# The last pair of heads in a streaming encoder layer: branch B first, branch A last, with the last gates split between them

## The chip, the cores and the metric

The kernel runs on one core of one Trainium2 chip. The metric is device time in microseconds, from the first to the last instruction of one execution with what lies around it; a kernel's time is the median of its runs. The core has a matmul engine (TensorE, "PE" in the profile, with its weight loads as "PEld"), a vector engine (VectorE, "DVE"), an activation engine (ScalarE, "ACT"), a general engine (GpSimd, "POOL") and a queue engine (SyncE, "SP"), from which nearly all DMAs of this kernel are issued in order.

## The reference

The reference is one layer of a streaming encoder, for 2048 frames of a new stream (the prompt) and for 16 new frames of each of 8 running streams (the samples), whose 512 earlier frames lie in caches. All is float32.

```python
h, gate = adaln_modulate(x, c, norm_g, w_ada, b_ada)
qa, ka, va, za, qb, kb, vb, zb, ga, gb = project_inputs(h, w_in, pos)   # 4 x 512, 4 x 512, 2 x 1024 columns
# branch A: 4 heads; two softmaxes a head, over chunk-causal keys
p = softmax(mask(q1k1, q2k2) * 64 ** -0.5);  oa = (p[0] - lam * p[1]) @ va
# branch B: 8 heads; stick-breaking weights over strictly earlier keys
log_1m = where(mask, log_sigmoid(-z), 0)
log_a = log_sigmoid(z) + cumsum(log_1m, reverse=True) - log_1m
ob = where(mask, exp(log_a), 0) @ vb
# merge
ya = (rms_norm(oa, subln_g) * (1 - lam_init) * silu(za)) @ w_branch_a
yb = (ob * silu(zb)) @ w_branch_b
x = x + gate * ((sigmoid(ga) * ya + sigmoid(gb) * yb) @ w_out)
y = rms_norm(x, final_g)
```

Keys and values of both branches are outputs too. Queries and keys of branch A are rotated by position.

## The kernel before

The 2048 prompt frames are 16 tiles of 128 rows (`t` from 0 to 15); the 8 x 16 sample frames make a seventeenth tile, `NT`. Each float32 factor of a large product is split into two float16 parts, high and low, and three products of parts stand for one: a projection of a tile is 3 x 8 matmuls.

The start normalizes the frames and writes the transposed parts to `hT_d`. The first part of the kernel then runs over eight *units*. Unit `u` has a head index `h` and a kind: kind 0 is one head of branch A, kind 1 is a pair of heads of branch B. `prepare_unit` sets these at line 326 as `h, kind = u // 2, u % 2`, so A and B take turns and unit 7 is a B unit. A unit goes over the tiles in the order `NT`, 0, ..., 15 (`steps`). For each step `project` (matmuls at line 452) makes 512 columns of queries, keys, values and the gate path `z`. A unit may also have a slice of the 2048 merge gates `ga`, `gb` (`gate_piece`, line 528); `GATES` at line 63 gives the units 1, 3, 5 and 7, which are the B units, 512 columns each, and none to the A units. The result goes to `g_d`.

`scores` issues the attention of a tile. Branch A: scores (681, 682, the mask at 685) are scaled on DVE with a running maximum (582), Exp runs on ACT with the sum (128), DVE joins the two softmaxes (635), ACT and DVE split the weights into a high (306) and a low half (311), and a transposing DMA (604) turns them for the product with the values (738 to 740). Branch B: ACT makes two sigmoids of the scores (128), DVE runs a scan along the keys, last chunk first (658), POOL multiplies (664), ACT casts the high half (596), DVE subtracts for the low half (597), and the same DMA turns them for lines 742 and 743. B has two such jobs a tile, A one. For A `store` sums squares of the output into `osums`.

The order of the work is written out by the loop over `steps`. Projections are a list of pieces, `line`; at each step, the loop takes pieces up to a position that grows with the estimated time of the attention done so far (`duration`) and leads it by five steps (`LEAD`), and lays them between the score chunks. So the first tiles of a unit are projected while the last tiles of the unit before are scored, and after the last projection some tiles of attention are left. Products with values are issued later by a lag (`later_on`, `give`). A scheduler in the framework may still move instructions against its own model of time. The call `act` keeps ACT's table functions (Exp, Sigmoid) in the written order.

Beside this go side pieces: the preparation of the next unit's weights (`back`; fetch, sum of squares, split), norms of other weights and cached values (`spare`), cached keys (`cached`) and, in unit 7, cuts of the branch weights. A cached key block (32 of them, 512 KB each) is fetched, squared on ACT, split by POOL and DVE (`halve`) and stored to `keys_d`; one stage of this pipeline is a side piece. `keys_at` at line 1004 allows them in tiles 0 to 7 of units 1, 3 and 5 and in tiles 9 to 12 of units 2, 4 and 6, one at a step. Weights and blocks share one list of 16 buffers of 4 KB a partition, `free`. A unit with 512 gate columns holds eight of them, one without gates four.

`early_work` prepares the first two tiles of the second part near the end of unit 7: `inputs` loads outputs, gate paths and gates, takes the reciprocal roots of `osums` (all 16 tiles at once, the first time it is called) and applies sigmoids. The second part runs over the tiles 0 to 14, `NT`, 15: branch matmuls (1428), transposes (1265), the output matmuls (1457), the last norm and the store. Beside the first 13 of them the sampled streams' attention runs, unit by unit (`sample`, `lane`).

```python
    def keys_at(u, t):
        return u in (1, 3, 5) and t < 8 or u in (2, 4, 6) and 9 <= t < 13
```

Of the kernel before, what the change touches and what calls it, by code (L numbers as in the profile page):

```python
# [26 lines left out]
P = 128  # L27
# [6 lines left out]
NT = SEQ // P  # L34
# [27 lines left out]

GATES = [(u // 2 * 512, u % 2 * 512) for u in range(8)]

# [54 lines left out]
def layer_kernel(ctx: ExitStack, tc: tile.TileContext, a: dict):  # L119
# [63 lines left out]
    con = ctx.enter_context(tc.tile_pool(name="con", bufs=1))  # L183
# [139 lines left out]
    def prepare_unit(u, keep=None):  # L323


        h, kind = u // 2, u % 2
        U = dict(h=h, kind=kind, u=u, w=[], wg=[], bufs=[])
# [559 lines left out]
    def norms():  # L887
# [49 lines left out]

        def stages(k):
            if k > 1:
                halve()  # L940
            if 0 < k <= len(todo):
                square()
            if k < len(todo):
                fetch(*todo[k])

        return [lambda k=k: one(k) for k in range(len(srcs) + 1)], [lambda k=k: stages(k) for k in range(len(todo) + 2)]

# [53 lines left out]
    def norm_at(u, t):  # L1001
        return u < 7 and t < NT and (t >= 7 if u == 0 else t >= 9 or u == 6)

    def keys_at(u, t):
        return u in (1, 3, 5) and t < 8 or u in (2, 4, 6) and 9 <= t < 13

# [245 lines left out]
    L = {}  # L1252
# [8 lines left out]
    def transposed(x16, dst, half):  # L1261
# [4 lines left out]
        S.copy(out=dst[:, half * KT : (half + 1) * KT, :], in_=pt.rearrange("p (k n) -> p k n", n=P))  # L1266

    def inputs(t):

# [9 lines left out]
        begun.append(t)  # L1279
        r = L["orms"][:, 4 * t : 4 * t + 4] if t < NT else rsqrt(osums[:, NT, :], 4, P, tiny, "rA")  # L1280
        G.tensor_tensor(out=o[:, 0:nz], in0=o[:, 0:nz], in1=z[:, 0:nz], op=ALU.mult)  # L1281
# [51 lines left out]
    def early_work():  # L1333


        free.extend(units[7]["bufs"])

        def first(t):
            if "orms" not in L:
                L["orms"] = rsqrt(osums[:, 0:NT, :].rearrange("p t h -> p (t h)"), 4 * NT, P, con, "orms")  # L1340
            states[t] = inputs(t)
            if t == tiles[0]:
                turned(states[t])
                opened(states[t])

        def rest():
            L["g"], L["u"], (L["y"], L["y16"]) = free[0:4], free[4:6], free[6:8]

        return [branch_weight for _ in branch_weights] + [rest] + [lambda t=t: first(t) for t in tiles[0:2]]

    for n in range(len(steps) + 2):
        made, qk, side = [], [], []
        if n < len(steps):
# [6 lines left out]
            for fn in back[: -(-len(back) // max(1, (W_READY if u else W_READY + 2) - t % NT))]:  # L1360
                side.append((1.0, back.pop(0)))
            for todo, here in ((spare, norm_at), (cached, keys_at)):
                if todo and here(u, t):
# [179 lines left out]
```

## Time and profile before

| | |
|---|---|
| median of 3 runs | 2275.9 us (2274.01 to 2279.74) |
| profiled execution, its own time | 2280.78 us |
| its span | 2279.0 us |
| mean granted PE clock | 0.97 |
| PE / PEld busy | 92% / 49% |
| DVE / ACT / POOL busy | 75% / 71% / 31% |
| DMA moved | 445.30 MB, mean 195 GB/s |

A group's row gives line, engine, operation, what it writes and reads with its shapes, the count, then busy time in us and the mean in ns of one, then the idle time of the engine just before and what ended it. A row of stretches gives the window, its length, busy time and count for each engine, the granted clock of PE as a share of full speed, the busy share of the DMA engines and GB/s; restricted to one line of the kernel, it gives that line's instructions alone. A row in order of time gives the start, the length, engine, line and operation; a bracket at its end tells how long the engine was idle before and what it waited for. A busy PE isn't PE at its peak: matmuls overlap, so the pitch of their starts tells more than the mean of one.

### The profile page before, as it was taken

The page shows a single profiled execution, that of the slowest core. Times are in us where ns is not written, and L with a number is a line of the kernel's source. Part 1 is how long each engine was busy: PE and PEld are TensorE (multiplying, and loading weights), DVE is VectorE, ACT ScalarE, POOL GpSimd, SP SyncE. Part 2 cuts the span into 40 slices and gives each one's busy share as a digit, 9 for nine tenths or more (in the row PEclk, how much of TensorE's full clock was granted, in tenths as well). Part 3 has the DMA queues.
Part 4 walks back from the last instruction along what each step waited for, and adds up shares of the span by engine and source line. Part 5 has one row for each costly group of instructions (what it writes and reads, how often), then busy time and mean ns, then how long its engine had stood idle before and what let it go on. Part 6 is the DMA issues. An engine that isn't in the chain of part 4 may idle for free. (4 is left out here: it accounts for less than half of the span.)

```text
span 2279.0 us, 41771 instructions
## 1 busy us (share of the span) xinstructions
PE 2086.9 (92%) x14752; PEld 1122.3 (49%) x14752; DVE 1716.8 (75%) x3795; ACT 1617.6 (71%) x3228; POOL 701.4 (31%) x610
## 2 busy tenths in 40 slices
PE   5998899999999899899999989998997789899998
PEld 3654455554555455455554545554553444444443
DVE  4658768778886787988688788877778777767753
ACT  3967777888887687888677788866778566556541
POOL 1223014446411444642044355302335212211211
PEclk8999999999999999999999999999998799999999
DMA  9777658998796999978888899655677899888321
GB/s 329 271 234 186 160 134 213 197 222 193 201 244 155 221 210 196 211 195 215 193 213 204 200 217 230 172 130 138 153 156 155 203 292 239 221 214 224 122 106 47
DMA packets 805827, 445.30 MB, mean 195 GB/s; under 512 B 537354, under 2 KB 744506, under 8 KB 805104
## 3 DMA queue, kind: packets, MB, share of 16 engines
q1 hardware_dynamic: 804668, 442.24, 78.5%
q8 instruction: 115, 1.88, 0.3%
q14 instruction: 96, 0.79, 0.1%
q10 hardware_dynamic: 948, 0.39, 0.1%
HBM read 228.82 MB, written 86.02 MB: 138 GB/s over the span
## 5 line engine op out<-in xcount | busy, mean ns | idle before, releaser
L664 POOL TENSOR_TENSOR sc_p<-sc_p,sc_n 128x127 f32<-128x127 f32 (+7 forms) x192 | 319.2, 1664 | 701.7 <-DVE sc_n L658 529.6
L452 PEld LDWEIGHTS <-hs 128*128 128x128 f16 x3120 | 293.4, 99 | 332.4 <-DMA hs<-hT_d 15.5
L452 PE MATMUL ps_mm<-wa,hs 128*128 128x512 f16 x1590 | 389.8, 384 | 9.5 <-DMA hs<-hT_d 8.6
L452 PE MATMUL ps_mm<-wb,hs 128*128 128x512 f16 x1530 | 376.9, 381 | 5.8 <-DMA hs<-hT_d 4.8
L528 PE MATMUL ps_t<-wb,hs 128*128 128x512 f16 x1224 | 290.7, 380 | 1.3 <-DVE qst L556 1.0
L658 DVE TENSOR_TENSOR_SCAN sc_n<-ps_s,sc_n,zero_t 128x512 f32<-128x512 f32 x192 | 245.4, 1278 | 48.9 <-ACT ps_s L128 44.2
L681 PE MATMUL ps_s<-k,qst 128*128 128x512 f16 (+3 forms) x640 | 226.0, 354 | 46.3 <-DVE sc_n L658 31.3
L597 DVE TENSOR_TENSOR sc_n<-sc_p,sc_n 128x128 f16<-128x128 f32 (+7 forms) x192 | 212.6, 1111 | 49.3 <-ACT sc_n L596 49.2
L128 ACT ACTIVATE sc_p<-ps_s,usc 128x512 f32<-128x512 f32 (+3 forms) x320 | 204.7, 640 | 61.5 <-PE ps_s L682 48.4
L528 PEld LDWEIGHTS <-hs 128*128 128x128 f16 x1632 | 156.5, 98 | 184.1 <-DVE qst L556 3.4
L682 PE MATMUL ps_s<-k,qst 128*128 128x512 f16 (+3 forms) x640 | 226.0, 354 | 0.0
L596 ACT CAST sc_n<-sc_p 128x128 f16<-128x128 f32 (+7 forms) x192 | 155.3, 814 | 68.6 <-POOL sc_p L664 68.0
L128 ACT ACTIVATE ps_s<-ps_s,usc 128x512 f32<-128x512 f32 (+3 forms) x328 | 199.6, 609 | 0.0
L1457 PE MATMUL ps_o<-wo,wb 128*128 128x512 f16 x816 | 182.9, 379 | 0.7 <-ACT wb L1266 0.7
L742 PE MATMUL ps_o<-v,wt 128*128 128x128 f16 x1088 | 131.4, 224 | 18.8 <-DMA wt<-sc_n 18.7
L582 DVE TENSOR_SCALAR_CACHE_REDUCE sc_n<-ps_s,usc 128x512 f32<-128x512 f32 (+3 forms) x160 | 106.4, 665 | 46.5 <-PE ps_s L685 30.8
L1457 PEld LDWEIGHTS <-wb 128*128 128x128 f16 x816 | 78.1, 98 | 94.5 <-issue 1.2
L738 PE MATMUL ps_o<-v,wt 128*128 128x128 f16 x544 | 100.4, 222 | 25.8 <-DMA wt<-sc_n 25.6
L743 PE MATMUL ps_o<-v,wt 128*128 128x64 f16 x1088 | 123.6, 197 | 0.0
L658 DVE TENSOR_TENSOR_SCAN sc_n<-ps_s,zero_t 128x128 f32<-128x128 f32 (+3 forms) x128 | 104.0, 813 | 25.5 <-ACT ps_s L128 24.9
L742 PEld LDWEIGHTS <-wt 128*128 128x128 f16 x1088 | 101.1, 101 | 44.2 <-DMA wt<-sc_n 24.8
L582 DVE TENSOR_SCALAR_CACHE_REDUCE sc_p<-ps_s,usc 128x512 f32<-128x512 f32 (+3 forms) x160 | 106.2, 664 | 21.3 <-PE ps_s L682 14.2
(369 smaller groups left out, 4425.7 us busy)
## 6 DMA issues: line engine op xcount, KB each, us to landing
hs<-hT_d SPq DMA_DIRECT2D x130, 512.0 KB, 4.4
g_d<-gt SPq DMA_DIRECT2D x68, 256.0 KB, 4.8
out_dram<-pr SPq DMA_DIRECT2D x204, 64.0 KB, 4.0
wa<-in_w_in_dram SPq DMA_DIRECT2D x34, 256.0 KB, 5.6
o_d<-o SPq DMA_DIRECT2D x136, 64.0 KB, 1.9
wa<-g_d SPq DMA_DIRECT2D x17, 512.0 KB, 5.5
wb<-g_d SPq DMA_DIRECT2D x17, 512.0 KB, 4.8
hs<-o_d SPq DMA_DIRECT2D x17, 512.0 KB, 5.5
```

The lines of the kernel that those rows point to most:

```text
L128: i = S.activation(**kw)
L452: T.matmul(box["p"], box["h"][:, hi, k, :], U["w"][k][:, wi, :], start=(n == 0), stop=(n == 3 * KT - 1))
L528: T.matmul(box["g"][:, 0:gw], box["h"][:, hi, k, :], U["wg"][k // per][:, k % per, wi, :], start=(j == 0), stop=(j == 3 * KT - 1))
L582: V.tensor_scalar(out=dst[:, lo : lo + n], in0=p[:, 0:n], scalar1=sc_pos, scalar2=None, op0=ALU.mult, op1=ALU.max, accum_out=job["mx"][:, ...
L596: S.copy(out=hi, in_=src)
L597: V.tensor_tensor(out=lo, in0=src, in1=hi, op=ALU.subtract)
L658: V.tensor_tensor_scan(out=dst[:, lo : lo + n][:, ::-1], data0=src[:, 0:n][:, ::-1], data1=zero_t[:, 0:1].to_broadcast([P, n]), initial=fi ...
L664: G.tensor_tensor(out=p[:, 0:m], in0=p[:, 0:m], in1=n[:, 1 : m + 1], op=ALU.mult)
L681: T.matmul(p[:, 0:n], qst[:, c, :], kk[:, c, 0:n], start=True, stop=False)
L682: T.matmul(p[:, 0:n], qst[:, 2 + c, :], kk[:, c, 0:n], start=False, stop=not diag)
L742: T.matmul(po[:, c * P : (c + 1) * P], wt[:, wj, :], vt[:, c, :, :], start=first, stop=False)
L1457: T.matmul(po, st["y"][:, yi * 8 + k, :], wo[j * 4 + k // 2][:, wi, k % 2, :], start=(n == 0), stop=(n == 3 * KT - 1))
```

## The change

Three tables replace three rules. `UNITS` gives head and kind of each unit; it differs from the rule before in the last two, where unit 6 is now the B pair of head index 3 and unit 7 the A head 3. `GATES` now gives, in units 6 and 7, 256 columns each of the last 512 gate columns; units 1, 3 and 5 keep 512. With 256 columns `prepare_unit` puts four slices of the weights in one staged buffer instead of two, and a unit holds six buffers. `KEYS_AT` replaces `keys_at` with five stretches, (unit, first tile, tile after the last): the 32 key blocks are dealt out as 7, 6, 7, 6, 6, and each stretch fills and empties its own pipeline, `n + 2` stages laid evenly over its tiles. Unit 5 has no stretch any more, and that of unit 6 lies in tiles 0 to 7.

Since the sums of unit 7 are now those of branch A, `inputs` takes the reciprocal roots from `roots`, in two groups of eight tiles, each computed when its first tile is prepared. The sampled streams' units follow `units`, so there too the last two change places.

```diff
-GATES = [(u // 2 * 512, u % 2 * 512) for u in range(8)]
+KEYS_AT = [(1, 0, 8), (2, 9, 13), (3, 0, 8), (4, 9, 13), (6, 0, 8)]
+UNITS = [(0, 0), (0, 1), (1, 0), (1, 1), (2, 0), (2, 1), (3, 1), (3, 0)]
+GATES = [(0, 0), (0, 512), (512, 0), (512, 512), (1024, 0), (1024, 512), (1536, 256), (1792, 256)]
...
-        h, kind = u // 2, u % 2
+        h, kind = UNITS[u]
...
-        def stages(k):
+        def stages(n, k):
             if k > 1:
                 halve()
-            if 0 < k <= len(todo):
+            if 0 < k <= n:
                 square()
-            if k < len(todo):
-                fetch(*todo[k])
...
+            if k < n:
+                fetch(*todo.pop(0))
+
+        halved = {}
+        for i, (u, first, last) in enumerate(KEYS_AT):
+            n = -(-len(todo) * (i + 1) // len(KEYS_AT)) - -(-len(todo) * i // len(KEYS_AT))
+            for k in range(n + 2):
+                halved.setdefault((u, first + k * (last - first) // (n + 2)), []).append(lambda n=n, k=k: stages(n, k))
...
-    def keys_at(u, t):
-        return u in (1, 3, 5) and t < 8 or u in (2, 4, 6) and 9 <= t < 13
...
+    def roots(t):
+
+        g = t // 8
+        if ("orms", g) not in L:
+            L["orms", g] = rsqrt(osums[:, g * 8 : g * 8 + 8, :].rearrange("p t h -> p (t h)"), 32, P, con, f"orms{g}")
+        return L["orms", g][:, t % 8 * 4 : t % 8 * 4 + 4]
...
-        r = L["orms"][:, 4 * t : 4 * t + 4] if t < NT else rsqrt(osums[:, NT, :], 4, P, tiny, "rA")
+        r = roots(t) if t < NT else rsqrt(osums[:, NT, :], 4, P, tiny, "rA")
...
-            if "orms" not in L:
-                L["orms"] = rsqrt(osums[:, 0:NT, :].rearrange("p t h -> p (t h)"), 4 * NT, P, con, "orms")
             states[t] = inputs(t)
...
-            for todo, here in ((spare, norm_at), (cached, keys_at)):
+            side += [(1.0, fn) for fn in cached.pop((u, t), [])]
+            for todo, here in ((spare, norm_at),):
```

More of the change, by code (lines that the diff above doesn't have):

```diff
@@ L936, in norms @@
         todo = [(name, h, i) for name in ("ak", "bk") for h in range(4) for i in range(4)]
-        def stages(k):
+        def stages(n, k):
             if k > 1:
                 halve()
-            if 0 < k <= len(todo):
+            if 0 < k <= n:
                 square()
-            if k < len(todo):
-                fetch(*todo[k])
-        return [lambda k=k: one(k) for k in range(len(srcs) + 1)], [lambda k=k: stages(k) for k in range(len(todo) + 2)]
+            if k < n:
[5 more added lines that the diff above has]
+                halved.setdefault((u, first + k * (last - first) // (n + 2)), []).append(lambda n=n, k=k: stages(n, k))
+        return [lambda k=k: one(k) for k in range(len(srcs) + 1)], halved
     steps = [(u, t) for u in range(8) for t in [NT] + list(range(NT))]
```

## The prediction

> **What bounds the kernel now.** I read the page first, then the tail of the eighth unit in order of time, then busy time by stretches, then groups by shape.
>
> ```profile
> span 2279.0 us, 41771 instructions
> ...
> PE 2086.9 (92%) x14752; PEld 1122.3 (49%) x14752; DVE 1716.8 (75%) x3795; ACT 1617.6 (71%) x3228; POOL 701.4 (31%) x610
> ```
>
> PE is the bound as a whole. Where it isn't, time can be won. To cut the span into units of attention I use ACT's table loads: one stands where Exp (branch A) follows Sigmoid (branch B) or the reverse. The row of 1552.25 ends unit 6 (A) and starts unit 7 (B).
>
> ```profile
> 1384.86 1.28 ACT L128 ACT_TABLE_LOAD   x1
> ...
> 1552.05 0.19 ACT L128 ACTIVATION_READ_ACCUMULATOR sc_n<-sc_n,nm 128x1 f32 x1
> 1552.25 1.28 ACT L128 ACT_TABLE_LOAD   x1
> 1553.55 0.31 ACT L128 ACTIVATE r<-szs 128x128 f32<-128x128 f32 x1
> ```
>
> ```profile
> core 0: us, PE busy (x) PEld busy (x) DVE busy (x) ACT busy (x) POOL busy (x), PEclk, DMA share, GB/s
> 967.30:1137.50 170.20, 165.14 (x1146) 90.47 (x1144) 134.27 (x380) 132.33 (x298) 38.83 (x44) 0.98 0.82 202
> 1137.50:1384.90 247.40, 231.03 (x1669) 125.00 (x1668) 202.13 (x338) 195.09 (x404) 120.49 (x94) 0.99 0.91 207
> 1384.90:1552.30 167.40, 160.12 (x1122) 87.32 (x1119) 133.73 (x373) 126.57 (x289) 36.82 (x41) 1.00 0.71 172
> 1552.30:1727.20 174.90, 167.74 (x1159) 89.46 (x1158) 133.99 (x226) 121.87 (x256) 60.10 (x50) 0.99 0.69 153
> 1727.20:1771.70 44.50, 28.72 (x238) 15.95 (x236) 41.75 (x51) 36.95 (x64) 27.83 (x15) 0.73 0.71 144
> 1771.70:1792.50 20.80, 8.04 (x97) 7.48 (x97) 16.58 (x29) 11.64 (x16) 6.64 (x5) 0.60 0.79 162
> ```
>
> These are units 4 (A), 5 (B), 6 (A), and 7 (B) in three pieces: up to its last projection matmul, up to its last score matmul ("tail"), up to the first matmul of the second part ("drain"). Up to 1727.2 PE idles 5 to 16 us in a unit. In the tail DVE is busy 41.75 of 44.5 us (94%) while PE is granted 0.73 of its clock and idles: three tiles of B's attention are left and no projection to lay beside them. In the drain PE waits for transposes:
>
> ```profile
> 1725.70 1.46 PE L528 MATMUL ps_t<-wb,hs 128*128 128x512 f16 x6
> ...
> 1771.33 0.38 PE L682 MATMUL ps_s<-k,qst 128*128 128x512 f16 x1
> 1773.12 0.23 PE L742 MATMUL ps_o<-v,wt 128*128 128x128 f16 x1 [1.41 <-DMA wt<-sc_n]
> ...
> 1777.75 0.29 PE L742 MATMUL ps_o<-v,wt 128*128 128x128 f16 x1 [3.78 <-DMA wt<-sc_n]
> ...
> 1788.24 0.29 PE L742 MATMUL ps_o<-v,wt 128*128 128x128 f16 x1 [4.84 <-DMA wt<-sc_n]
> ...
> 1792.50 0.97 PE L1428 MATMUL ps_mm<-wa,wb 128*128 128x512 f16 x3
> ```
>
> So I add up five pieces: 247.4 + 167.4 + 174.9 + 44.5 + 20.8 = 655.0 us.
>
> **The change, part by part.** Prices of one operation:
>
> ```profile
> L658 DVE TENSOR_TENSOR_SCAN sc_n<-ps_s,sc_n,zero_t 128x512 f32<-128x512 f32 x192 | 245.4, 1278 | 48.9 <-ACT ps_s L128 44.2 <-DVE sc_n L658 0.5
> ...
> L597 DVE TENSOR_TENSOR sc_n<-sc_p,sc_n 128x1024 f16<-128x1024 f32 x80 | 118.0, 1475 | 28.6 <-ACT sc_n L596 28.5
> ...
> L582 DVE TENSOR_SCALAR_CACHE_REDUCE sc_n<-ps_s,usc 128x512 f32<-128x512 f32 x112 | 83.4, 745 | 22.4 <-PE ps_s L682 14.6 <-PE ps_s L685 7.0 <-DMA wt<-sc_n 0.6
> ...
> L635 DVE SCALAR_TENSOR_TENSOR sc_p<-sc_n,r,sc_p 128x1024 f32<-128x1024 f32 x40 | 51.7, 1296 | 0.0
> ...
> L311 DVE SCALAR_TENSOR_TENSOR sc_n<-sc_p,r,sc_n 128x1024 f16<-128x1024 f32 x40 | 51.7, 1292 | 4.5 <-ACT sc_n L306 4.5
> ...
> L306 ACT ACTIVATE sc_n<-sc_p,r 128x1024 f16<-128x1024 f32 x40 | 46.2, 1154 | 27.7 <-DVE sc_p L635 27.3
> ...
> L128 ACT ACTIVATE sc_p<-sc_p,nm 128x1024 f32<-128x1024 f32 x40 | 45.8, 1145 | 40.2 <-DVE nm L614 40.1
> ...
> L311 DVE SCALAR_TENSOR_TENSOR wa<-wa,csc,wa 128x1024 f16<-128x1024 f32 x24 | 37.4, 1558 | 8.3 <-POOL wa L308 8.3
> ...
> L128 ACT ACT_TABLE_LOAD x15 | 19.2, 1283 | 0.2
> ```
>
> *Tail.* For the last tile B needs on DVE 8 scans and 4 subtractions: 8 x 1.278 + 4 x 1.475 = 16.1 us. A needs 8 evacuations, 2 joins and 2 low halves: 8 x 0.745 + 2 x 1.296 + 2 x 1.292 = 11.1 us. The ratio is 0.69, so the tail of 44.5 becomes 30.5 us. ACT isn't the new bound: 4 exponentials and 2 high halves are 4 x 1.145 + 2 x 1.154 = 6.9 us a tile. A also sends one job of transposes a tile instead of two, so SP has half as many to issue there. Ends: 26 us if A's DVE work runs without a gap beside the shorter queue (1.5 us off each of three tiles), 44.5 if something other than DVE held the tail. I take 30.5 since DVE's 94% leaves room for little else.
>
> *Drain.* After A's last evacuation come four exponentials (4.6), join (1.3), high half (1.2), low half (1.3), a transpose (4.3 to landing, the median of its row below) and the second segment behind it (1.3): about 14 us, then 24 blocks of products. The first two tiles of the second part are prepared in the same stretch, as before, and their sigmoids stand between A's exponentials in ACT's fixed order, so tables are switched there: Exp to Sigmoid, back, and again, where B's Sigmoid needed none. One switch is 1.28 us by its rows, with the neighbours within 0.02 us on both sides. If the three lie on the path the drain is 14 + 2 + 3.8 = 20, if none does 16; I take 18 against 20.8, since the first falls under the last evacuations. The Trainium skill, "ScalarE: Activation LUTs", section "What ACT_TABLE_LOAD costs", adds a drain of about 1.4 us to the load's 1.28 us; by that the drain would end near 20 and the whole change would bring 2 us less. The rows of 1384.86 and 1552.25 show no such second part.
>
> ```profile
> wt<-sc_n SPq DMA_TRANSPOSE x288, 4.3
> ```
>
> *Gates.* 17 tiles x 24 matmuls of 512 columns become twice as many of 256. Pitches:
>
> ```profile
> 2161.52 5.19 PE ps_mm L1428 x24
> ```
>
> ```profile
> 1000.93 0.27 PE L681 MATMUL ps_s<-k,qst 128*128 128x256 f16 x1
> 1001.04 0.27 PE L682 MATMUL ps_s<-k,qst 128*128 128x256 f16 x1
> ```
>
> 0.216 and 0.11 us: 816 x 0.11 - 408 x 0.216 = +1.6 us of PE in all. ACT gets 17 more evacuations, SP 17 more stores of gates; both have room (below). The weights are fetched in the same bytes, with two staged blocks for each half instead of four for one.
>
> *Where PE's work goes.* By line the projections of the three units stand so (446, 375 and 267 matmuls), and 512-column gates 288, 109 and 301:
>
> ```profile
> 1137.50:1384.90 247.40, 109.38 (x446) 42.11 (x446) 0.99 0.91 207
> 1384.90:1552.30 167.40, 88.32 (x375) 35.05 (x375) 1.00 0.71 172
> 1552.30:1727.20 174.90, 65.00 (x267) 24.66 (x267) 0.99 0.69 153
> ```
>
> ```profile
> 1137.50:1384.90 247.40, 66.73 (x288) 27.49 (x288) 0.99 0.91 207
> 1384.90:1552.30 167.40, 24.80 (x109) 10.49 (x110) 1.00 0.71 172
> 1552.30:1727.20 174.90, 70.97 (x301) 28.88 (x299) 0.99 0.69 153
> ```
>
> Unit 5: (446 - 288) / 24 = 6.6 tiles of unit 6 are projected beside it, each now with gates: 158 x 0.11 = +17.4 us of PE. Against that go eight blocks of cached keys (on DVE a low half of 1.56 us and four tiny operations, some 2 us each), and DVE's share falls to that of the A units, where PE idles 5 to 7 us instead of 16. 231 + 17.4 + 7 - 2 (less half clock) = 253 us. Ends: 248 (no idle) and 265 (idle as before). I take 253.
>
> Unit 6, now B: 408 projections and 408 half gates, 133 us at the pitches above, with a unit's own scores and products, 62 us (231.0 - 734 x 0.216 = 72.5 in unit 5's row, 160.1 - 484 x 0.216 = 55.6 in unit 6's; the mean, less 2 of half clock): PE 195. DVE: unit 5's 202, less eight blocks of keys (16), plus six (12), less 3 that lie between its last score and the table load: 195; ACT, with two squares fewer, about 192. POOL's load becomes that of unit 5's row, half of the time; unit 7 takes over the rotations of A's queries and keys and keeps room, and SP issues 48 transposes in unit 6 for 24. Three engines at nearly the same load; this is the doubtful term. The nearest stretch is B's last tiles beside projections without gates:
>
> ```profile
> 1330.00:1410.00 80.00, 70.86 (x539) 38.48 (x538) 71.93 (x122) 66.49 (x139) 48.83 (x44) 0.96 0.97 204
> ```
>
> DVE is at 90% there. 195 / 0.90 = 217 us against 167.4. Ends: 202 (PE with an A unit's 7 us of idle) and 239 (DVE at unit 5's 82%).
>
> Unit 7, now A: the remaining 234 projections and 250 half gates, 78 us, with 42 us of products and scores up to the tail (167.7 - 568 x 0.216 = 45 in its row, less an estimated 3 since A's late products came over from unit 6 and B's are fewer), and 6 of idle: 126 us. DVE has room.
>
> *Keys.* The 32 blocks and their loads and stores on SP are the same, in 42 stages for 34, since each stretch fills and empties itself. Unit 5 loses its eight (counted above). Units 2 and 4 get six blocks in four tiles where they had four: two stages a tile. There PE already waits once:
>
> ```profile
> 1050.00:1065.00 15.00, 10.95 (x72) 6.22 (x70) 9.74 (x27) 11.26 (x28) 1.22 (x1) 0.77 0.96 228
> ```
>
> DMA is at 0.96 in this stretch. I count the crowding at nothing, as PE is full in the next tiles and DMA stands at 0.82 over the unit; without that cover it is 4 us in each of two units.
>
> *Reciprocal roots.* They are computed for eight tiles at a time: 15 small DVE operations twice. The first set waits for sums of tiles 0 to 7 of the last unit, stored several tiles before; what stands behind it on DVE is the preparation of the second part's first tile, which PE needs only after the drain. The second set lies in the second part, some 3 us of DVE beside PE. Counted at nothing; at most 3 us. Order of the sampled streams' units: the last two change places, the same work.
>
> *Sum.* 253 + 217 + 126 + 30.5 + 18 = 644.5, against 655.0: 10.5 us less. The profiled execution took 2280.78 us (span 2279.0), 4.9 above the median of 2275.9; the difference carries over to the median: 2265.
>
> **The rivals.**
> 1. Slower: unit 6 is held by DVE and ACT. If DVE reaches only the 82% of unit 5's row, the unit takes 239 us and the sum is 11.5 over the present: 2287. For it: B's scan, POOL multiply, ACT cast and subtraction form one chain, and PE no longer has the long gates that cover it. Against: 90 to 94% where DVE was the bound. It decides from 227 us (86%), and shows as slower from 234 us on.
> 2. No change: the idle of unit 5 stays at 16 us (+9), because it comes from small tiles' latency and late loads, not from DVE. Then 2274. Crowded keys would lead to the same place (+8).
> 3. More: unit 6 runs like an A unit, PE-bound at 202 us: 2250.
>
> **How the numbers follow.** Likeliest 0.45, its own range 2259 to 2271; rival 1 0.2, rival 2 0.2, rival 3 0.15. What this measurement can tell from no change is about 0.3%, 6.8 us: faster means below 2269. The likeliest case lies there but for a tenth, and all of rival 3: 0.56; with rival 2 and the rest, same 0.22; slower 0.22. The range that leaves out 2 in 10 goes from 2250 to 2286, the last just short of rival 1's point.
>
> **What would show it.** The stretch from the last projection matmul to the last score matmul should be near 30 us, with evacuations (L582) instead of scans; the drain 16 to 20 us with two or three table loads; no table load between units 5 and 6; from the load that opens unit 5 to the one before unit 7 some 470 us, and PE idle there of 25 to 30 us. The forecast is wrong if that span is over 485, if DVE waits for ACT and POOL in unit 6, or if the tail isn't shorter though DVE has less to do.

## The result and the profile after

The changed kernel takes 2297.1 us (median of six runs, 2292.8 to 2302.7) against 2275.9 us: a ratio of 1.0093, 95% interval 1.0073 to 1.0112. It is slower by about 21 us, where 2265 us (2250 to 2286) was forecast. The profiled execution took 2301.77 us, its span 2300.0, with a mean granted PE clock of 0.964 for 0.970. Lines of the first part stand two further down than before (line 682 is now 684), lines of the second part by five or more (1428 is 1439).

The page of the kernel after, span and busy time:

```profile
span 2300.0 us, 42681 instructions
...
PE 2107.5 (92%) x15162; PEld 1172.9 (51%) x15162; DVE 1714.3 (75%) x3817; ACT 1622.6 (71%) x3246; POOL 688.3 (30%) x611
```

The page hardly differs: 408 of the 410 more matmuls are the halved gates, and PE is busy 20.6 us longer while the span grew by 21. "Busy" counts a matmul at half clock as a long one, so this is no sign of more work. The stretches show the place. First the kernel before, busy time by stretches for units 2 and 3, which the prediction did not show (length, then busy time and count on PE, PEld, DVE, ACT and POOL, granted clock, DMA share, GB/s):

```profile
551.90:720.50 168.60, 163.05 (x1147) 89.54 (x1148) 133.50 (x379) 131.50 (x299) 38.52 (x43) 1.00 0.82 204
720.50:967.30 246.80, 228.87 (x1654) 123.66 (x1653) 201.84 (x336) 195.27 (x404) 119.33 (x93) 0.99 0.91 205
```

The same view of the kernel after: units 2, 3 and 4, units 5 and 6 together, then unit 7 up to its last projection matmul, its tail and the drain:

```profile
551.40:735.60 184.20, 171.20 (x1150) 92.96 (x1151) 137.47 (x390) 133.76 (x303) 39.83 (x45) 0.95 0.80 198
735.60:982.50 246.90, 230.74 (x1648) 124.48 (x1645) 199.43 (x332) 194.70 (x400) 116.11 (x92) 0.99 0.89 200
982.50:1165.90 183.40, 171.93 (x1172) 94.10 (x1173) 139.27 (x392) 135.72 (x308) 39.75 (x46) 0.97 0.80 194
1165.90:1620.50 454.60, 429.12 (x3320) 256.87 (x3318) 378.26 (x620) 366.04 (x760) 202.06 (x157) 0.98 0.84 191
1620.50:1775.70 155.20, 140.42 (x1104) 89.48 (x1102) 104.62 (x293) 90.09 (x214) 36.31 (x42) 0.97 0.56 135
1775.70:1794.70 19.00, 11.99 (x84) 7.16 (x83) 17.49 (x42) 13.64 (x25) 1.27 (x1) 0.91 0.51 127
1794.70:1813.40 18.70, 6.09 (x54) 5.25 (x53) 14.84 (x38) 18.46 (x23) 0.00 (x0) 0.52 0.38 82
```

Unit 2 went from 168.6 to 184.2 us (+15.6) and unit 4 from 170.2 to 183.4 (+13.2). Unit 3 did not move. Units 5 to 7 fell from 655.0 to 647.5 (-7.5), and the second part is the same, 486.5 and 486.6 us. 15.6 + 13.2 - 7.5 = 21.3. So by the stretches the swap and the split of gates, on which the forecast spent its terms, are not where the time came from: it came from the two units whose cached keys now run two stages a tile.

The 7.5 us aren't idle time that was filled. PE is busy 8.0 us less in units 5 to 7 (587.6 for 595.7), because matmuls run elsewhere: unit 4 holds 26 more than before (1172 for 1146), and the second part 98 more (3177 for 3079, busy 448.1 us for 440.0).

Unit 2 has nearly the same matmuls as before (1150 and 1147), but PE idles 13.0 us instead of 5.6 and is busy 8.2 us longer at a granted clock of 0.95 for 1.00. In stretches of 10 us around the stages of keys, the kernel before:

```profile
630.00:640.00 10.00, 8.29 (x64) 4.83 (x61) 8.76 (x28) 9.22 (x25) 1.33 (x1) 1.00 1.11 286
640.00:650.00 10.00, 8.77 (x80) 5.48 (x78) 7.78 (x22) 8.79 (x24) 1.22 (x1) 1.00 0.90 219
650.00:660.00 10.00, 10.00 (x49) 4.57 (x48) 9.45 (x25) 8.56 (x20) 1.12 (x1) 1.00 0.76 184
660.00:670.00 10.00, 9.99 (x81) 5.74 (x80) 10.00 (x33) 8.12 (x20) 1.12 (x1) 1.00 1.01 258
```

and after:

```profile
631.00:641.00 10.00, 8.56 (x73) 5.19 (x72) 8.52 (x31) 6.66 (x15) 2.56 (x3) 1.00 0.85 180
641.00:651.00 10.00, 6.39 (x39) 3.65 (x38) 5.66 (x16) 5.62 (x14) 1.12 (x1) 0.88 1.07 261
651.00:661.00 10.00, 7.23 (x40) 3.98 (x39) 8.16 (x23) 9.90 (x25) 1.12 (x1) 0.67 0.80 215
661.00:671.00 10.00, 10.00 (x72) 5.57 (x70) 6.63 (x20) 6.20 (x14) 2.24 (x2) 0.94 0.97 229
671.00:681.00 10.00, 6.33 (x37) 3.13 (x34) 6.03 (x15) 5.49 (x15) 0.00 (x0) 0.92 0.81 247
681.00:691.00 10.00, 9.89 (x52) 4.64 (x52) 5.84 (x20) 4.72 (x10) 1.12 (x1) 0.74 0.93 236
```

DMA is loaded about alike. What is new is that PE, DVE and ACT go slack together (in the stretches from 641 and from 671), and that the granted clock falls to 0.67 to 0.94 behind the gaps. All three waiting at once suggests that one thing is late for all. The order of time on SP's queue and on ACT (the bracket gives the idle time before an instruction and what ended it):

```profile
640.35 0.43 SPq L914 DMA_DIRECT2D wa<-in_cache_a_k_dram  x1
```

```profile
645.38 1.06 ACT L288 ACTIVATE junk<-wa 128x1024 f16<-128x1024 f32 x1 [5.11 <-DMA wa<-in_cache_a_k_dram]
```

The block of keys is issued at 640.35, and ACT, whose order is fixed, stands 5.11 us before its square. Behind the square on ACT are the casts and copies from which PE's next transposes and scores start. The waits of the stretch 631 to 691 (what waited, for what, total, times, longest):

```profile
ACT junk L288 <- DMA wa<-in_cache_a_k_dram: 5.1, 1, 5.1
...
ACT junk L288 <- DMA wb<-in_cache_a_v_dram: 2.7, 1, 2.7
...
PE ps_s L227 <- ACT junk L288: 3.4, 2, 2.6
...
PE ps_s L683 <- DVE csc L926: 2.6, 1, 2.6
```

Line 227 is the small matmul that adds a block's sums of squares over the partitions; it stands in PE's order, so PE waits for the square too. Line 683, a score, waits for line 926, which reads that sum out of `ps_s`, the buffers that the scores are written to. The load, the square, the sum and its reading form one chain through SP's queue, ACT, PE and DVE, each in its order. Before, neither of PE's two waits stood in unit 2; but ACT waited for loads of blocks there too, in the stretch 616 to 676:

```profile
ACT junk L286 <- DMA wa<-in_cache_a_k_dram: 3.7, 3, 1.9
```

So the chain is seen, and PE's waits in it (3.4 + 2.6 us) are new. How much of the 28.8 us hangs on the late load, the experiments have to tell.

### The profile page after: what moved, and what is told of

It is laid out like the page before. It is cut to its first block, busy times and chain, and to the rows that moved or that the text cites. A ratio compares the mean times of both kernels' runs of the same rounds, so it can differ in the third digit from the quotient of the medians.

```text
span 2300.0 us, 42681 instructions
## 1 busy us (share of the span) xinstructions
PE 2107.5 (92%) x15162; PEld 1172.9 (51%) x15162; DVE 1714.3 (75%) x3817; ACT 1622.6 (71%) x3246; POOL 688.3 (30%) x611
## 5 line engine op out<-in xcount | busy, mean ns | idle before, releaser
L666 POOL TENSOR_TENSOR sc_p<-sc_p,sc_n 128x127 f32<-128x127 f32 (+7 forms) x192 | 309.3, 1614 | 612.7 <-DVE sc_n L660 580.9
L454 PEld LDWEIGHTS <-hs 128*128 128x128 f16 x3120 | 294.2, 99 | 333.1 <-issue 17.2
L454 PE MATMUL ps_mm<-wb,hs 128*128 128x512 f16 x1530 | 377.1, 384 | 13.3 <-DMA hs<-hT_d 13.2
L530 PE MATMUL ps_t<-wb,hs 128*128 128x512 f16 (+1 forms) x1530 | 295.2, 341 | 1.5 <-ACT qst L558 0.9
L530 PEld LDWEIGHTS <-hs 128*128 128x128 f16 x2040 | 198.6, 99 | 158.5 <-issue 12.2
L495 POOL TENSOR_TENSOR rot<-pr,rope 128x256 f32<-128x256 f32 x68 | 55.6, 817 | 280.8 <-ACT pr L468 141.6
L740 PE MATMUL ps_o<-v,wt 128*128 128x128 f16 x544 | 106.3, 230 | 28.5 <-DMA wt<-sc_n 28.4
```

What stands on the lines that cost most here:

```text
L454: T.matmul(box["p"], box["h"][:, hi, k, :], U["w"][k][:, wi, :], start=(n == 0), stop=(n == 3 * KT - 1))
L530: T.matmul(box["g"][:, 0:gw], box["h"][:, hi, k, :], U["wg"][k // per][:, k % per, wi, :], start=(j == 0), stop=(j == 3 * KT - 1))
L666: G.tensor_tensor(out=p[:, 0:m], in0=p[:, 0:m], in1=n[:, 1 : m + 1], op=ALU.mult)
```

## The experiments

Stage lengths below are of one profiled execution each, between table loads and the marks of the prediction. Where the code of a stretch is the same they differ by some 3 us (unit 2 in after and keys_only, or in late_b and late_swap; units 5 to 7 in after, spread and quarter), and by up to 10 us in the second part (482 to 493). Ratios are to the kernel before on the same chip.

A stretch doesn't hold the same matmuls in every kernel, since projections move across its ends. So the last two columns give an estimate of what is left of units 2 and 4 without them, called net: the length less the time of the stretch's own matmuls at the pitches that these traces show at full clock (0.216 us for 512 columns, 0.162 for 384, 0.109 for 256, 0.056 for 128, 0.028 for 64).

| kernel | ratio, 95% interval | unit 2 | unit 4 | 5+6 | 7 with tail and drain | 5 to 7 | unit 2 net | unit 4 net |
|---|---|---|---|---|---|---|---|---|
| before | 1 | 168.6 | 170.2 | 414.8 | 240.2 | 655.0 | 8.1 | 10.0 |
| after | 1.0093 [1.0073, 1.0112] | 184.2 | 183.4 | 454.6 | 192.9 | 647.5 | 24.1 | 18.8 |
| keys_only | 1.0071 [1.0047, 1.0095] | 181.4 | 182.5 | 411.8 | 235.1 | 646.9 | 21.3 | 17.8 |
| spread | 1.0068 [1.0044, 1.0092] | 176.3 | 181.6 | 457.8 | 192.9 | 650.7 | 16.3 | 21.6 |
| split_noswap | 1.0106 [1.0083, 1.0129] | 175.3 | 179.0 | 445.2 | 215.8 | 661.0 | 15.4 | 19.0 |
| swap_nosplit | 1.0271 [1.0244, 1.0298] | 175.0 | 180.4 | 467.7 | 232.4 | 700.1 | 15.0 | 20.4 |
| quarter | 1.0035 [1.0022, 1.0047] | 172.6 | 175.7 | 459.9 | 191.0 | 650.9 | 13.7 | 15.7 |
| no_norms | 1.0072 [1.0048, 1.0095] | 179.5 | 178.8 | 478.9 | 182.5 | 661.4 | 14.1 | 12.4 |
| four | 1.0070 [1.0051, 1.0089] | 171.2 | 178.7 | 462.0 | 194.5 | 656.5 | 11.3 | 19.0 |
| b_only | 1.0014 [0.9998, 1.0030] | 165.7 | 161.7 | 476.7 | 180.2 | 656.9 | 8.3 | 5.0 |
| prefetch | 1.0055 [1.0038, 1.0072] | 174.0 | 171.1 | 474.1 | 181.3 | 655.4 | 14.4 | 11.4 |
| late_b | 1.0056 [1.0043, 1.0069] | 170.8 | 177.6 | 421.9 | 235.9 | 657.8 | 11.2 | 18.5 |
| late_b3 | 1.0051 [1.0031, 1.0071] | 165.9 | 164.5 | 420.9 | 237.3 | 658.2 | 8.5 | 7.0 |
| late_swap | 1.0035 [1.0022, 1.0047] | 173.9 | 176.7 | 470.1 | 181.7 | 651.8 | 14.1 | 17.6 |

By the last columns the change costs 16.0 us in unit 2 and 8.8 in unit 4 beyond the matmuls; the other 4.3 us of unit 4 are matmuls that moved there (164.6 us at the pitches for 160.3).

The theory after the first look: the crowded stages of keys cost what was lost, and swap with split is worth a few us at most. The rival: swap and split shift work and the loss in units 2 and 4 is a by-product of something else, such as another order from the scheduler.

### keys_only: the keys and the roots without the swap and the split

```diff
-UNITS = [..., (2, 0), (2, 1), (3, 1), (3, 0)]
-GATES = [..., (1536, 256), (1792, 256)]
+UNITS = [..., (2, 0), (2, 1), (3, 0), (3, 1)]
+GATES = [..., (1536, 0), (1536, 512)]
```

> The kernel before with only the five stretches of cached keys (and the roots in two groups); order of units and gates as before. Theory C (crowding: two key stages a tile in units 2 and 4 cost 13 to 15 us each): about 28 us slower than before, ratio 1.012, with the attention of units 2 and 4 (from Exp's table load to the next one) at 183 us each against 169 and 170. Rival O (the new order and the split are what costs): within 5 us of before, ratio 1.000 to 1.002, both units near 170 us.

Busy time by stretches of this kernel: units 2, 4, 5 and 6, and unit 7 up to its last projection.

```profile
553.00:734.40 181.40, 168.17 (x1150) 91.63 (x1151) 137.50 (x390) 133.73 (x304) 39.79 (x45) 0.96 0.82 201
...
980.40:1162.90 182.50, 172.74 (x1174) 94.88 (x1175) 139.12 (x393) 135.60 (x308) 39.95 (x46) 0.96 0.81 195
1162.90:1397.90 235.00, 222.27 (x1611) 120.20 (x1609) 187.70 (x294) 185.76 (x381) 108.39 (x85) 0.99 0.84 186
1397.90:1574.70 176.80, 164.77 (x1144) 90.60 (x1145) 139.08 (x407) 132.72 (x298) 42.67 (x46) 0.99 0.71 187
1574.70:1746.10 171.40, 166.79 (x1156) 88.99 (x1155) 131.81 (x226) 121.59 (x255) 61.78 (x50) 0.99 0.70 156
```

Units 2 and 4 lose 12.8 and 12.3 us with no swap and no split anywhere, near the 183 us that the theory expected, and the rival is out. The rest is a trade: unit 5, rid of its eight blocks, gains 12.4, unit 6, to which six come, loses 9.4, and unit 7 gains 5.1 in all. So the kernel isn't the expected 28 us slower, but 16. In units 5 to 7 it takes 646.9 us and the full change 647.5: swap and split together bring nothing measurable. The keys alone account for a ratio of 1.0071 of the 1.0093; the intervals overlap.

### spread: the stages of units 2 and 4 over eight tiles

```diff
-KEYS_AT = [(1, 0, 8), (2, 9, 13), (3, 0, 8), (4, 9, 13), (6, 0, 8)]
+KEYS_AT = [(1, 0, 8), (2, 5, 13), (3, 0, 8), (4, 5, 13), (6, 0, 8)]
```

> The changed kernel with the stretches of units 2 and 4 in tiles 5 to 12 instead of 9 to 12, so one key stage a tile; the same blocks, buffers, order and gates. Theory C: the 28 us of units 2 and 4 go, units 2 and 4 back near 170 us each, 2268 us, ratio 0.997. Rival O: still near 2297, ratio 1.009. A third way, that any key work beside those A units costs by its amount and not by its pace (six blocks instead of four): units 2 and 4 at 175 to 180 us, ratio about 1.004.

Six blocks at one stage a tile give 176.3 and 181.6 us: 7.9 us back in unit 2, 1.8 in unit 4. Net, unit 2 gets 7.8 of its 16.0 us back and unit 4 none (21.6 for 18.8). So the pace is part of it in unit 2 alone, and a theory that puts everything down to the pace fell short. Six blocks, spread over eight tiles, still cost more than the four before. The next two kernels stand on this one.

### split_noswap and swap_nosplit: the two other parts, one without the other

```diff
-UNITS = [..., (3, 1), (3, 0)]
+UNITS = [..., (3, 0), (3, 1)]
```

> As spread, but with A in unit 6 and B in unit 7 as before, 256 gate columns each. This isolates the order of the units: if the shorter tail of A is the gain, this kernel keeps B's tail and drain (65 us against 38 in the changed kernel) and is some 5 to 15 us slower than spread, near or above before. If the gain came from the split alone, it is within 4 us of spread.

Here unit 6 is A and unit 7 is B as before, each with 256 columns of gates. Units 5, 6 and 7 up to the last projection, and the tail:

```profile
1155.90:1395.70 239.80, 230.21 (x1674) 128.71 (x1673) 186.88 (x296) 185.51 (x382) 106.82 (x81) 0.99 0.84 182
1395.70:1601.10 205.40, 195.21 (x1511) 123.89 (x1509) 147.12 (x415) 139.65 (x318) 44.26 (x50) 0.98 0.70 173
1601.10:1748.00 146.90, 135.73 (x1140) 89.26 (x1138) 131.02 (x224) 116.57 (x254) 64.94 (x50) 0.98 0.77 163
1748.00:1796.50 48.50, 31.74 (x262) 19.45 (x261) 43.03 (x52) 38.04 (x67) 28.16 (x15) 0.69 0.72 145
```

Against keys_only, unit 5 grows by 4.8 us and unit 6, to which the gates moved, by 28.6; the body of unit 7 is shorter by 24.5, its tail longer by 4.5. DVE is busy 131.0 of the body's 146.9 us (89%): this B unit, with less PE work, comes near DVE's pace. So the split costs about 14 us in units 5 to 7 (661.0 against 646.9). Of these, 4.7 are matmuls that keys_only has done in unit 4, and the two kernels differ in the keys of units 2 and 4 too, so the split by itself wasn't measured.

```diff
-GATES = [..., (1536, 256), (1792, 256)]
+GATES = [..., (1536, 0), (1536, 512)]
```

> As spread, but the last 512 gate columns lie whole in unit 7 (now A) and unit 6 (now B) has none. If DVE's load in unit 6 is what makes the split worth having, unit 6 loses PE work that it could have hidden: units 5 and 6 together shorter by some 44 us less what DVE holds (DVE's 378 us at 90% make 420), unit 7 longer by 53; 8 to 20 us slower than spread. If the split doesn't matter, the same as spread within 4 us.

Here unit 6 is B without gates and unit 7 is A with all 512 columns. Units 5 and 6:

```profile
1150.90:1618.60 467.70, 414.49 (x2970) 223.40 (x2967) 379.57 (x617) 364.64 (x750) 202.81 (x155) 0.94 0.80 181
```

PE has 20 us less to do in units 5 and 6 than in the spread kernel (414.5 for 434.9) and they still take 9.9 us longer, with 53 us of idle PE at a clock of 0.94. PE waits there 18.8 us for transposes of B's attention weights and 15.7 us for the scan (line 660), where it waits 4.1 and 3.8 in the spread kernel. So the chain of branch B sets unit 6; PE work taken out of it is not time taken out, and in unit 7 it has to be done after all (232.4 us for 192.9). That is 2.0% more than the spread kernel, some 46 us where 8 to 20 were expected. The swap needs the split. On top of the split the swap gains 10 us (650.7 against 661.0, both with spread keys; by the ratios 0.4%), and the split costs up to 14: so the two nearly cancel.

### quarter: the loads of units 2 and 4 cut to a quarter

```diff
-            src = caches[name][:, i * 8 : i * 8 + 8, h * P : (h + 1) * P]
-            load(out=st.rearrange("p (j n) -> p j n", n=P), in_=src)
+            src = caches[name][:, i * 8 : i * 8 + m, h * P : (h + 1) * P]
+            load(out=st.rearrange("p (j n) -> p j n", n=P)[:, 0:m, :], in_=src)
...
-                fetch(*todo.pop(0))
+                fetch(*todo.pop(0), 2 if u in (2, 4) else 8)
```

> The changed kernel with the loads of the cached key blocks of units 2 and 4 cut to a quarter (128 KB for 512 KB); every instruction on ACT, DVE, POOL, PE and every issue stays. It leaves out three quarters of the data of these twelve blocks, so their stored keys and sums aren't the reference's. If the bytes of the loads are the cost (DMA share 0.9 to 1.1 in the stretch, late landing), units 2 and 4 fall to 170 to 175 us; if the cost is instructions in order on the engines or the stores, they stay at 180 or more.

Every stage, square, sum and store is as in the full change, at the same crowded pace; only 2 of 8 slices of the twelve blocks are fetched. Units 2 and 4:

```profile
555.60:728.20 172.60, 164.28 (x1135) 89.93 (x1133) 139.62 (x390) 133.79 (x303) 39.28 (x46) 0.98 0.79 197
974.00:1149.70 175.70, 166.63 (x1150) 92.31 (x1151) 138.94 (x389) 133.95 (x303) 38.68 (x45) 0.97 0.78 189
```

11.6 and 7.7 us come back, 19 of the 28.8. Part of it is fewer matmuls (1135 and 1150 for 1150 and 1172); net it is 10.4 and 3.1 us of 16.0 and 8.8, about half. So the bytes of the loads cost something, in unit 2 above all, and the rest stays without them. The time to landing was hardly tried here: ACT waits 6.5 and 9.7 us for loads before its squares in the two units, 7.8 and 9.9 in the full change. The next two kernels leave the blocks' bytes as they are.

### no_norms and prefetch: the other loads away, and the blocks fetched earlier

```diff
-        return u < 7 and t < NT and (t >= 7 if u == 0 else t >= 9 or u == 6)
+        return u < 7 and t < NT and (t >= 7 if u == 0 else t >= (13 if u in (2, 4) else 9) or u == 6)
```

> The changed kernel, crowded stretches kept, but the norms of other weights and cached values (one 512 KB load and one ACT square a tile) taken out of tiles 9 to 12 of units 2 and 4 and done later. If the crowding costs through shared loads and the short list of buffers (a load that waits on the SP queue for a buffer just stored), most of it goes: units 2 and 4 at 170 to 175 us instead of 184 and 183. If it costs because a block's square stands on ACT behind its own late load, units 2 and 4 stay at 180 or more.

The norms of cached values, which are loaded, squared and summed beside the stages, are put off to other tiles. Units 2 and 4, and 5 with 6:

```profile
551.40:730.90 179.50, 170.52 (x1201) 94.47 (x1199) 139.81 (x393) 130.22 (x296) 42.74 (x46) 0.99 0.79 194
970.90:1149.70 178.80, 170.29 (x1215) 94.33 (x1216) 137.68 (x393) 130.12 (x296) 42.57 (x46) 1.00 0.77 190
1149.70:1628.60 478.90, 434.02 (x3290) 255.82 (x3288) 385.50 (x625) 375.72 (x780) 205.17 (x157) 0.96 0.86 190
```

Only 4.7 and 4.6 us come back, which fits neither of the two expectations. But the two stretches hold 51 and 43 matmuls more than in the full change (1201 and 1215), so more work is done in them, and unit 3, for instance, falls to 240.0 us. Net, 10.0 of 16.0 us come back in unit 2 and 6.4 of 8.8 in unit 4: two thirds of the loss hang on the norms that stand beside the keys in the same tiles. The kernel gains little from it, since the eight norms that landed in units 5 and 6 cost 24 us there (478.9 for 454.6), of which unit 7 gives back 10: that stretch has little slack for side work. The prefetch kernel keeps this and fetches each block of units 2 and 4 two stages ahead of its square instead of one.

```diff
-        def stages(n, k):
-            if k > 1:
+        def stages(n, k, d):
+            if k > d:
                 halve()
-            if 0 < k <= n:
+            if d - 1 < k <= n + d - 1:
                 square()
...
+            d = 2 if u in (2, 4) else 1
...
+        halved.setdefault((2, 8), []).insert(0, flush)
+        halved.setdefault((4, 8), []).insert(0, flush)
```

> As no_norms, but in units 2 and 4 a block is loaded two stages ahead of its square instead of one (same bytes, same engine work, one stage more to empty). If what remains of the crowding there (179 us a unit) is the lateness of a block's own load, with ACT's square waiting for it in order, units 2 and 4 fall to 171 to 174 us. If it is the bandwidth or the amount of work, they stay at 178 to 180.

`flush` finishes a pending norm, so that it doesn't stand in the way. The same two units:

```profile
552.40:726.40 174.00, 165.27 (x1146) 91.72 (x1147) 138.04 (x389) 129.42 (x295) 41.03 (x46) 0.98 0.79 198
973.40:1144.50 171.10, 162.72 (x1146) 89.72 (x1147) 137.60 (x389) 129.12 (x294) 41.49 (x45) 1.00 0.78 195
```

The two units are 5.5 and 7.7 us shorter than in no_norms, as if the lateness of the load were the cause. The rows say otherwise: PE idles 8.7 and 8.4 us in them, as it did in no_norms (9.0 and 8.5), and they hold 55 and 69 matmuls fewer. That work is done in other stretches (unit 3 takes 247.0 us again for 240.0). Net the two kernels are the same in both units, 14.4 and 11.4 us for 14.1 and 12.4. So fetching a block earlier brought nothing measurable here, and the ratios, 1.0055 and 1.0072, have overlapping intervals. This kernel also differs from no_norms by `flush` and was run on another chip.

### four, b_only, late_b, late_b3, late_swap: where can 32 blocks lie?

```diff
-            n = -(-len(todo) * (i + 1) // len(KEYS_AT)) - -(-len(todo) * i // len(KEYS_AT))
+            n = (8, 4, 8, 4, 8)[i]
```

> The changed kernel with the blocks dealt 8, 4, 8, 4, 8 instead of 7, 6, 7, 6, 6: units 2 and 4 get four blocks in four tiles, as many as before, but in stretches that fill and empty themselves (six stages in four tiles). If the number of blocks in the stretch is what costs, units 2 and 4 come back to 170 to 173 us and the kernel to about 2275, ratio 1.000; if filling and emptying is what costs, they stay near 180.

Four blocks instead of six in units 2 and 4 take unit 2 to 171.2 us and unit 4 to 178.7, and the kernel to 1.0070 and not 1.000. Unit 2 answers as if the number of blocks were the cost, unit 4 as if filling and emptying were: net it keeps all of its loss (19.0 for 18.8), though ACT waits for no block's load there. Unit 1, with eight blocks for seven, went from 242.5 to 248.3, and units 5 and 6 from 454.6 to 462.0. The kernel before has eight blocks in unit 1 too, fetched in eight stages instead of ten, and takes 241.1 us for it. So filling and emptying each stretch by itself has a price of its own.

```diff
-KEYS_AT = [(1, 0, 8), (2, 9, 13), (3, 0, 8), (4, 9, 13), (6, 0, 8)]
+KEYS_AT = [(1, 0, 13), (3, 0, 13), (6, 0, 13)]
```

> The changed kernel with all cached keys in the B units, stretches over tiles 0 to 12 of units 1, 3 and 6 (11, 11 and 10 blocks), none in units 2 and 4. If key work is cheap in long B units (some 1.5 us a block, as between unit 5 with and without keys: 247 and 235 us) and dear in short A units: units 2 and 4 at 165 us or below, unit 3 at 250, units 5 and 6 up by some 6 us together; 2262 to 2270 us, ratio 0.994 to 0.998. If keys cost the same anywhere, 2297 as the changed kernel.

Ten or eleven blocks in each of three B units and none in the A units. Units 2, 3 and 4, and 5 with 6:

```profile
559.40:725.10 165.70, 160.29 (x1123) 88.50 (x1124) 127.13 (x358) 127.45 (x290) 32.13 (x39) 0.99 0.78 182
725.10:978.30 253.20, 235.23 (x1682) 127.87 (x1680) 208.35 (x353) 199.33 (x409) 117.14 (x96) 0.98 0.91 212
978.30:1140.00 161.70, 158.25 (x1115) 86.83 (x1114) 128.41 (x359) 127.60 (x291) 34.13 (x40) 1.00 0.75 180
1140.00:1616.70 476.70, 436.56 (x3377) 259.94 (x3374) 391.45 (x648) 372.84 (x773) 215.42 (x161) 0.98 0.86 192
```

Units 2 and 4 fall below the kernel before, by 2.9 and 8.5 us, so the keys of units 2 and 4, and what stands with them, account for the loss there. It is paid in unit 3 (+6.4 over before), in unit 1 (249.0 for 241.1) and in units 5 and 6, 22 us over the full change, of which unit 7 gives back 13. 1.0014 can't be told from no change, where 0.994 to 0.998 was expected: this version of the change gives back the loss and no more.

The last three put the blocks into the later tiles of the B units, where PE's projections are thick. Two, late_b and late_b3, have the old order of units and the old gates, and so try the keys by themselves; late_swap keeps swap and split.

```diff
-KEYS_AT = [(1, 0, 8), (2, 9, 13), (3, 0, 8), (4, 9, 13), (6, 0, 8)]
+KEYS_AT = [(1, 5, 13), (2, 9, 13), (3, 5, 13), (4, 9, 13), (5, 5, 13)]
...
+            n = (8, 4, 8, 4, 8)[i]
```

> Order of units and gates as before the change; keys dealt 8, 4, 8, 4, 8 over units 1 to 5 as before, but in the B units in tiles 5 to 12 instead of 0 to 7. If key stages cost PE time because they fall into B's small early tiles (unit 5 took 247 us with them and 235 without, all of it in its first 90 us), units 3 and 5 come to about 238 each and the kernel to 2255 to 2262, ratio 0.991 to 0.994. If they cost the same in any tile, within 5 us of before.

```diff
-KEYS_AT = [(1, 0, 8), (2, 9, 13), (3, 0, 8), (4, 9, 13), (6, 0, 8)]
+KEYS_AT = [(1, 3, 14), (3, 3, 14), (5, 3, 14)]
...
```

> Order of units and gates as before the change; all key blocks in the B units, 11, 11 and 10 over tiles 3 to 13 of units 1, 3 and 5, none in A units. If a block costs little in B's later tiles: units 2 and 4 at 163 to 166 us, units 3 and 5 at 240 to 245, 2250 to 2260 us, ratio about 0.990. If a block costs 1.5 to 2 us wherever it lies, within 5 us of before.

```diff
-KEYS_AT = [(1, 0, 8), (2, 9, 13), (3, 0, 8), (4, 9, 13), (6, 0, 8)]
+KEYS_AT = [(1, 5, 13), (2, 9, 13), (3, 5, 13), (4, 9, 13), (6, 5, 13)]
...
+            n = (8, 4, 8, 4, 8)[i]
```

> The changed order and split gates, keys dealt 8, 4, 8, 4, 8 with the B units' stretches in tiles 5 to 12. Units 2 and 4 as in the run with four blocks (171 and 179 us), unit 3 down by 8 us if late tiles are cheap; unit 6 is bound by DVE, so its eight blocks cost 1.5 to 3 us each there whatever the tile. 2280 to 2292 us; slower than the same keys in the old order, if the order and the split together bring nothing.

Units 3 and 5 of late_b, then unit 3 of late_b3:

```profile
726.80:969.00 242.20, 228.62 (x1653) 124.00 (x1651) 199.88 (x332) 196.43 (x406) 113.10 (x92) 0.99 0.93 206
...
1146.60:1398.60 252.00, 232.03 (x1638) 125.41 (x1637) 203.70 (x330) 193.40 (x400) 108.46 (x92) 0.97 0.87 202
```

```profile
720.60:976.90 256.30, 236.53 (x1671) 127.10 (x1669) 208.48 (x352) 198.24 (x410) 121.39 (x97) 0.97 0.89 208
```

Neither of the times expected for the two kernels came: they are 14 and 11 us slower than before. The idea that the later tiles are a cheap place fell: unit 3 gains 4.6 us with its eight blocks there and unit 5 loses 4.6. In late_b3, with eleven blocks in unit 3, that unit takes 9.5 us more than before, while units 2 and 4, without any, gain 2.7 and 5.7. late_b keeps the old counts (8, 4, 8, 4, 8) and differs from before in A only by its pace, six stages in four tiles: unit 4 still takes 177.6 for 170.2 us, unit 2 170.8 for 168.6. late_swap is late_b with swap and split and its last eight blocks in unit 6. Its 651.8 us in units 5 to 7 are 6.0 fewer: with keys placed so, swap and split are worth that little; 4.7 of the 6.0 are matmuls that aren't done in these units, and the intervals of the two ratios just touch. No version tried is faster than the kernel before.

## Why the prediction was wrong

**The step that failed** is the last sentence on the keys: "I count the crowding at nothing, as PE is full in the next tiles and DMA stands at 0.82 over the unit; without that cover it is 4 us in each of two units." It measured 15.6 and 13.2 us, 28.8 for 0; net of matmuls that moved, 16.0 and 8.8, or 24.8. The value taken was wrong, and so was the upper end of 8. Two things in the working led there. The share of DMA over a unit (0.80 in both units now) says nothing of what happens in a few tiles: the block that ACT's square waited for was in flight for 5 us (640.35 to 645.38), which is short by itself and long when the square is next in ACT's order. And "PE is full in the next tiles" took PE as cover for a wait that stands in PE's own order (line 227) and in ACT's, ahead of the copies that feed PE. The end of 4 us was one such wait; there are six blocks a unit, and half clock followed the gaps (8.2 of unit 2's 15.6 us are longer matmuls). keys_only shows that no other part of the change is needed for it, and b_only that the loss goes with the keys. Inside the crowded tiles the cost is shared: of the 24.8 us, no_norms brings back 16.4 by taking the norms out, and quarter 13.5 by cutting the blocks' bytes; together that is more than the whole, so the two overlap. That the lateness of a block's own load is the larger part isn't shown; prefetch speaks against it. Neither pace nor count explains unit 4, which stays at 181.6 us in spread and 178.7 in four.

**Units 5 to 7 together** came out near the forecast, 647.5 for 644.5 us, and that is luck: the terms were off by -15.4, +29.2, -11.5 and +0.7 us. One by one:

- *Units 5 and 6*: 454.6 for 470. PE idle there is 454.6 - 429.1 = 25.5 us, inside the 25 to 30 named. The forecast laid 34 projections and 49 half gates more beside unit 6 than ran there: unit 7 issued 268 and 299 where 234 and 250 were counted. At 0.216 and 0.11 us that is 12.7 of the 15.4 us.
- *Unit 7 before the tail*: 155.2 for 126. The same 12.7 us came here. PE is busy 140.4 us, 7.6 more than the counts at the forecast's pitches with its 42 us of other work (132.8); about 5 of these are half clock (granted 0.97 over 155.2 us). Idle time is 14.8 for 6, of which 9.4 us are waits for loads of `hs`.
- *Tail*: 19.0 for 30.5, with evacuations in place of scans as foreseen. DVE sets it, as foreseen (17.49 busy of 19.0, 92%), but two tiles were left, 14 and 15, and not three: in the body DVE is busy 104.6 of 155.2 us, so A's attention keeps up with the projections.
- *Drain*: 18.7 for 18, with three table loads, and none between units 5 and 6, both as named. But the path was another. The first branch matmul doesn't wait for A's last products, which run behind it; it waits for the first tile of the second part, whose casts and copies stand on ACT behind the sigmoids, the exponentials and the table loads. ACT is busy 18.46 of the 18.70 us. PE after:

```profile
1810.39 1.03 PE L1270 MATMUL ps_s<-id,hs 128*128 128x128 f16 x8 [9.24 <-ACT hs L308]
...
1817.61 0.31 PE L740 MATMUL ps_o<-v,wt 128*128 128x128 f16 x1
```

- *Gates*: 0.11 us for 256 columns held (0.109 by the starts).

So a shorter end was won (tail and drain 65.3 to 37.7 us) and nearly all of it was paid back ahead of it. By the rows PE idles 59.4 us over units 5 to 7 before and 59.9 after: in tail and drain 28.5 before and 19.6 after, in the bodies 30.8 and 40.3. The idle time moved; it wasn't filled. keys_only, without swap and split, reaches the same 647 us. So the 7.5 us that units 5 to 7 gained are no worth of the new order.

**The rivals.** Rival 1 had the right sign with the wrong place: unit 6 as B is held by its own chain, as swap_nosplit shows, but hardly at 239 us. No table load parts units 5 and 6 any more; if unit 5 takes the 239.8 us of split_noswap, unit 6 takes some 215, near the 217 of the forecast (an estimate). Rival 2 named crowded keys at +8, less than a third of what they cost, and put them down as no change. Rival 3 didn't happen.

**What stays open.** Why unit 4 keeps its loss with four blocks (net 19.0 in four, 18.5 in late_b, 10.0 before) while unit 2 gives most of it back isn't known. Nor is how much of the crowding is lateness of loads: the wait of 5.11 us is seen, its worth isn't. Why the split costs up to 14 us in the old order was seen only by stages: a B unit near DVE's pace and a longer tail. How much of the lost time in the body of unit 7 comes from late loads, and how much from the copies of gates on ACT (which waits 22.1 us for line 530 there, by the waits), wasn't tried apart. Nor was what remained of the crowding with a quarter of the bytes.

## What to carry to other kernels

Price side work by its place, not by its total: twelve blocks instead of eight in two units of 170 us, beside norms that stood there already, cost 24.8 us beyond PE's own work, while DMA's share over the units didn't rise. Before an order of work is changed for a shorter tail, ask what covered the waits in the stages that give up their work; here they gave back what the tail had won. Test the parts of a change by themselves: the bookkeeping part, which looked free, was most of the loss (1.0071 of 1.0093). And compare stretches only at equal work: by length alone, prefetch seemed to win 13 us over no_norms, and PE's idle time in the two units was the same.

## What was unexpected in the hardware

By the lengths of its rows on SP, a transposing DMA holds the queue between 1.17 and 6.4 us for its issue (332 of them in the kernel after: median 1.8 us, 78 of them over 3 us; before it is the same, 76 of 332), and what stands behind it goes out so much later: behind the one of 643.59, which took 2.90 us, the next block's load was issued at 647.17. The prediction had counted only its time to landing.

PE needn't stand still to lose its clock. The records of the granted clock hold only 1 and 0.5, in steps of 3.41 us. In unit 2 after, half clock follows the steps from 645.19, 652.02 and 675.91 us, in which PE was busy 1.02, 1.30 and 0.59 us (30%, 38% and 17%); the step from 635.0, busy 1.96 us (58%), is followed by full clock. Over the whole kernel after, each of the 27 falls follows a step with PE busy about half of the time or less; where full clock was kept, PE had been busy at least 43% of the step.

The three table loads of the drain stand between Exp and Sigmoid without a gap, in the order of time on ACT after:

```profile
1794.18 0.18 ACT L130 ACTIVATION_READ_ACCUMULATOR sc_n<-sc_n,nm 128x1 f32 x1
1794.38 1.28 ACT L130 ACT_TABLE_LOAD   x1
1795.68 0.63 ACT L130 ACTIVATE hs<-hs 128x512 f32<-128x512 f32 x1
...
1799.46 1.28 ACT L130 ACT_TABLE_LOAD   x1
...
1805.40 1.28 ACT L130 ACT_TABLE_LOAD   x1
```

The neighbours end and start within 0.02 us, so a switch costs 1.3 us. The Trainium skill, "ScalarE: Activation LUTs", section "What ACT_TABLE_LOAD costs", adds a drain of about 1.4 us to it; these rows show none.
